# im2col on one core: the first load split by channel over the SyncE and the ScalarE queue, ahead of the opening barrier

## Chip, cores, metric

One core of one Trainium2 chip. The metric is device time in microseconds, the lower the better.

## The reference

The input is `x`, 16 images of 64 channels of 32x32 float32. For each image, channel and tap (ki, kj) of a 3x3 window, the output row holds the 30x30 shifted plane:

```python
for i in range(h_out):            # 30
    for j in range(w_out):        # 30
        patch = x[b, :, i:i + 3, j:j + 3]
        cols[b, :, i * w_out + j] = patch.ravel()      # cols: 16 x 576 x 900
```

There is no arithmetic, only copies. 4.19 MB are read and 33.18 MB written.

## The kernel before

1024 channels lie on 128 partitions, eight channels on each. Four pairs of channels are expanded one after the other into an output tile (two buffers) by VectorE and ScalarE, and each pair goes out as one store of 8.3 MB.

```python
    def load(r0, r1):
        return nc.sync.dma_start(out=in_flat[:, r0 * W : r1 * W],
                                 in_=x_v[:, r0 * W : r1 * W])

    first = load(0, 2 * H)        # channels 0 and 1: 8192 bytes per partition
    load(2 * H, CPP * H)          # channels 2 to 7: 24,576 bytes per partition
    ...
    for c in range(0, CPP, 2):    # four pairs
        out_tile = out_pool.tile([P, 2, KK, HO, WO], x.dtype, name="out_tile")
        for s in range(2):
            ...                   # ScalarE: taps 3..5 (and 8 if s == 1); VectorE: the rest
        nc.sync.dma_start(out=..., in_=...)     # 64,800 bytes per partition
    ...
    # after compilation: 'first' is moved ahead of SyncE's drain in the opening barrier
```

## Time and profile before

| | before |
|---|---|
| device time, median of 3 runs | 91.12 us |
| span in the profile (that run took 91.39 us) | 89.6 us |
| first packet starts, last store packet ends | 1.01 us, 88.33 us |
| first pair of channels: copies start | 4.93 us |
| first store issued | 10.69 us |

The span runs from the first to the last instruction; device time is 1.8 us more.

A landing is counted from the issue and includes the time in which a transfer stands behind others. Where the text speaks of "packets", it means the trace's single DMA records: start, duration, queue and bytes of each. A row of one partition is one packet: the trace of before has 128 of either load and 512 of the stores, on the mean of the 16 DMA engines eight of each load and 32 store packets.

### The profile page before, as it was taken

Reading aid. Unit: us, or ns where it says so; the run is one execution under the profiler, and the core shown is the slowest. Engines: PE = TensorE matmul, PEld = TensorE weight load, DVE = VectorE, ACT = ScalarE, POOL = GpSimd, SP = SyncE. Lnnn points to the kernel's source line nnn. Section 1 sums busy time; section 2 is a strip of 40 time slices with the busy share of each in tenths; the row PEclk is TensorE's granted clock in tenths of the full one; section 3 lists DMA queues with packets and bytes.
Section 4 is the critical chain, followed back from the end, with each engine's and each line's share of the span. In section 5 each row is a group of like instructions: output and inputs, shape, how many; then the busy total and the mean of one; then the engine's idle time right before and its main releaser. Section 6 shows DMA issues by size and latency. Waiting matters only on the chain.

```text
span 89.6 us, 96 instructions
## 1 busy us (share of the span) xinstructions
DVE 22.6 (25%) x24; ACT 23.8 (27%) x13; POOL 0.2 (0%) x4
## 2 busy tenths in 40 slices
DVE  0079759900000099500000399100000000000000
ACT  5079759900000099500000399100000000000000
POOL 0000000000000000000000000000000000000000
DMA  5989899999999999947999999999999982999990
GB/s 128 505 384 494 362 463 463 463 463 463 463 463 463 463 463 463 434 174 318 463 463 463 463 463 463 463 463 463 463 463 463 463 347 116 463 463 463 463 463 0
DMA packets 864, 37.37 MB, mean 417 GB/s; under 512 B 96, under 2 KB 96, under 8 KB 96
## 3 DMA queue, kind: packets, MB, share of 16 engines
q1 hardware_dynamic: 864, 37.37, 97.2%
HBM read 4.19 MB, written 33.18 MB: 417 GB/s over the span
## 4 chain that ended last, share of the span: by engine, by line
DMA 49%; DVE 12%; DVEq 1%; issue 0%; SPq 0%
DMA out_dram<-out_tile 36%; DMA in_tile<-in_x_dram 13%; DVE out_tile L57 8%; DVE out_tile L61 2%; DVE out_tile L65 1%; DVEq L89 1%; DVEq L57 0%; SPq L71 0%
## 5 line engine op out<-in xcount | busy, mean ns | idle before, releaser
L55 ACT COPY out_tile<-in_tile 128x2700 f32<-128x2700 f32 x8 | 19.2, 2443 | 31.7 <-DMA out_dram<-out_tile 27.1
L57 DVE COPY out_tile<-in_tile 128x1800 f32<-128x1800 f32 x16 | 16.8, 1092 | 33.7 <-DMA out_dram<-out_tile 27.1
L61 DVE COPY out_tile<-in_tile 128x1800 f32<-128x1800 f32 x4 | 4.4, 1090 | 0.0
L68 ACT COPY out_tile<-in_tile 128x900 f32<-128x900 f32 x4 | 3.8, 938 | 0.0
L65 DVE COPY out_tile<-in_tile 128x900 f32<-128x900 f32 x4 | 2.5, 620 | 0.0
L55 ACT ACT_TABLE_LOAD x1 | 1.3, 1283 | 0.8 <-PEq L118 0.8
L118 POOL MEMSET const-bfloat16-1.0<- 128x1 bf16 x1 | 0.1, 101 | 0.0
L118 POOL MEMSET const-uint8-127<- 128x1 uint8 x1 | 0.1, 101 | 0.0
L118 POOL MEMSET const-float32-0.0<- 128x1 f32 x1 | 0.1, 98 | 0.2 <-issue 0.2
L118 POOL MEMSET const-float32-1.0<- 128x1 f32 x1 | 0.1, 98 | 0.0
## 6 DMA issues: line engine op xcount, KB each, us to landing
out_dram<-out_tile SPq DMA_DIRECT2D x4, 8100.0 KB, 32.4
in_tile<-in_x_dram SPq DMA_DIRECT2D x1, 3072.0 KB, 11.4
in_tile<-in_x_dram SPq DMA_DIRECT2D x1, 1024.0 KB, 4.9
```

The costliest lines, as they stand in the source:

```text
L55: nc.scalar.copy(out=o[:, K : 2 * K], in_=planes(c + s, 1, 0, K, 1))
L57: nc.vector.tensor_copy(out=o[:, ki * K : ki * K + 2], in_=planes(c + s, ki, 0, 2, 1))
L61: nc.vector.tensor_copy(out=o[:, 2:KK:6], in_=planes(c + s, 0, 2, 2, 2 * W))
L65: nc.vector.tensor_copy(out=o[:, 2], in_=in_tile[:, c + s, 0:HO, 2 : 2 + WO])
L68: nc.scalar.copy(out=o[:, 8], in_=in_tile[:, c + s, 2 : 2 + HO, 2 : 2 + WO])
L89: tc.compile()
L118: nc = _bacc.Bacc("TRN2", target_bir_lowering=False, num_devices=1)
```

## The change

The intent is to have channel 0 in SBUF earlier: two loads of 512 KB, on two queues, both out before the barrier, so that the copies and the first store can start sooner.

```diff
-    def load(r0, r1):
-        return nc.sync.dma_start(
+    def load(queue, r0, r1):
+        return queue.dma_start(
...
-    first = load(0, 2 * H)
-    load(2 * H, CPP * H)
+    first = load(nc.sync, 0, H), load(nc.scalar, H, 2 * H)
+    load(nc.sync, 2 * H, CPP * H)
...
-    load = first.ins
-    (moved ahead of the drain of its engine in the first block)
+    for load in (f.ins for f in first):
+        (the same, each ahead of the drain of its own engine)
```

More of the change, by code (lines that the diff above doesn't have):

```diff
@@ L90 @@
     blocks = tc.nc.main_func.blocks
-    load = first.ins
-    home = next(b for b in blocks if any(i.name == load.name for i in b.instructions))
-    home.instructions = [i for i in home.instructions if i.name != load.name]
-    head = list(blocks[0].instructions)
-    at = next(
-        k
-        for k, i in enumerate(head)
-        if i.engine == load.engine and type(i).__name__ == "InstDrain"
-    )
-    head.insert(at, load)
-    blocks[0].instructions = head
+    for load in (f.ins for f in first):
+        home = next(
+            b for b in blocks if any(i.name == load.name for i in b.instructions)
+        )
+        home.instructions = [i for i in home.instructions if i.name != load.name]
+        head = list(blocks[0].instructions)
+        at = next(
+            k
+            for k, i in enumerate(head)
+            if i.engine == load.engine and type(i).__name__ == "InstDrain"
+        )
+        head.insert(at, load)
+        blocks[0].instructions = head
 _INS = ['x', 'kernel_size']
```

## The prediction

> **What bounds the kernel now.** I read the page's busy shares first, then its DMA queue, then the chain of waits, and last the timeline of the first 18 us and the trace's single DMA packets, because the change touches only the first five microseconds.
>
> The queue table and the busy line say which resource is full:
>
> ```profile
> DVE 22.6 (25%) x24; ACT 23.8 (27%) x13; POOL 0.2 (0%) x4
> ...
> q1 hardware_dynamic: 864, 37.37, 97.2%
> HBM read 4.19 MB, written 33.18 MB: 417 GB/s over the span
> ```
>
> VectorE and ScalarE work a quarter of the span each; the 16 DMA engines are busy for 97.2% of it. That leaves 2.8% of 89.6 us, 2.5 us per DMA engine, in which no packet moves. This is all that any change of order can win. The packet records say where those 2.5 us lie. The first packet starts at 1.01 us (the 16 engines start one after the other until 1.39), the last store packet ends at 88.33, so about 1.0 to 1.4 us lie at the head and 1.27 at the tail. In between each engine works almost without a pause. The dips in the GB/s row near 40 and 74 us are no idle time: in the records a new row of 16 packets starts within 6 ns of the old one's end there.
>
> The one inner gap is between the loads and the first store. On the engine that is done first the second load ends at 11.25 us and its first store packet starts at 11.54, a gap of 0.29 us; on the last engine they are at 11.839 and 11.836, no gap. The mean over the 16 engines is about 0.18 us (loads end at 11.42 on average, stores start at 11.6).
>
> The timeline shows how the first store comes to be issued when it is:
>
> ```profile
> 0.00 1.12 SPq L35 DMA_DIRECT2D in_tile<-in_x_dram  x2
> ...
> 0.78 1.28 ACT L55 ACT_TABLE_LOAD   x1 [0.78 <-PEq L118]
> 4.93 4.79 ACT L55 COPY out_tile<-in_tile 128x2700 f32<-128x2700 f32 x2 [2.87 <-DMA in_tile<-in_x_dram]
> 4.93 2.10 DVE L57 COPY out_tile<-in_tile 128x1800 f32<-128x1800 f32 x2 [4.93 <-DMA in_tile<-in_x_dram]
> ...
> 9.63 0.94 ACT L68 COPY out_tile<-in_tile 128x900 f32<-128x900 f32 x1
> 9.97 0.62 DVE L65 COPY out_tile<-in_tile 128x900 f32<-128x900 f32 x1
> 10.69 7.60 SPq L71 DMA_DIRECT2D out_dram<-out_tile  x2
> ```
>
> Both engines wait for the first load until 4.93 and then work without a break until 10.57 (ScalarE) and 10.59 (VectorE). The store is issued at 10.69; its first packet follows 0.85 us later, at 11.54. The second load holds the DMA engines until 11.24 to 11.83 meanwhile. So the compute of the first pair of channels is already hidden under the second load, all but that gap of 0.29 us. The page's chain names the second load, and then the stores, as what ended last:
>
> ```profile
> DMA 49%; DVE 12%; DVEq 1%; issue 0%; SPq 0%
> DMA out_dram<-out_tile 36%; DMA in_tile<-in_x_dram 13%; DVE out_tile L57 8%; DVE out_tile L61 2%; DVE out_tile L65 1%; DVEq L89 1%; DVEq L57 0%; SPq L71 0%
> ```
>
> Its VectorE share is misleading: it lies under store packets (the compute of 50.6 to 56.3 us runs beside the third store). What sets the end is the packet stream, 32 store packets per engine at a pace of 2.395 us, 76.6 us, from 11.6 to 88.3.
>
> [...] 64,800 bytes each 2.395 us on 16 engines is 433 GB/s[...].
>
> **The change part by part.** It takes 4 KB per partition from the first load and gives them to the ScalarE queue. Bytes, copies and stores stay.
>
> *Packets.* Eight packets of 8192 bytes per engine, 306 ns apart, become sixteen of 4096. From the paces of 306 ns and 908 ns (24,576 bytes) a packet costs about 5 ns plus 36.7 ns per 1024 bytes, so 4096 bytes take about 155 ns (an estimate); 16 x 155 - 8 x 306 is +0.03 to +0.04 us on the stream.
>
> *Issue.* SyncE issues at 0.00 as before. ScalarE's first recorded instruction, the drain of the barrier, is at 0.13 us, so its load goes out near 0.13[...]. SyncE's own drain runs from 0.43 to 0.56 and lets the barrier go (second load at 0.79). ScalarE's drain then comes last, so the second load is issued at about 0.9 to 1.1. That costs nothing: the rings are full until after 3.5 us. The table load moves by as much and ends at 2.4 at the latest, before any data.
>
> *Landing of channel 0.* The data of both first loads take the same time together, to 3.98 to 4.56 us. If both rings fill at once and alternate, channel 0 is complete one packet before channel 1, so 0.15 us earlier than now. If ScalarE's packets come 0.3 us later, SyncE's ring leads by two or three packets, and channel 0 is complete some 0.3 to 0.5 us earlier. The copies start at about 4.5 to 4.8.
>
> *Landing of channel 1.* SyncE's ring goes straight on with packets of 24,576 bytes, 0.91 us each. [...] ScalarE needs it 2.35 us after its start, at 6.9 to 7.2; VectorE 3.03 us after. [...]
>
> *First store.* Its issue moves from 10.69 to between 10.2 and 10.7. What that is worth is capped by the gap, 0.18 us on average, since the second load ends no earlier. I take -0.08 us for it, +0.04 for the packets, and -0.03 for a start in which two first packets per engine overlap (now the first packet takes 0.51 to 1.15 us instead of 0.31). The sum is -0.07, so 91.12 becomes 91.05. One more semaphore in the closing waits falls in SyncE's idle time.
>
> **The rivals.**
>
> *Channel 1 is starved.* If the ScalarE ring starts a microsecond late, [...] Channel 1 then lands near 8.7 to 9, is visible near 9.2, ScalarE needs 3.3 us after that (2.35 + 0.94), and the store is issued at 12.5: its packets come at 13.4 instead of 11.6, and nothing fills the hole. This makes 92.5 to 93. For it: the order within SyncE's ring. Against it: ScalarE reaches the barrier at 0.13 us already, so it is not late.
>
> *Channel 0 really comes first.* If the rings are not served in turn but SyncE's first, channel 0 lands near 3.1 and the copies start 1.2 us earlier. The store is issued before 10, the gap closes fully, and the time is 90.9. Even this best case wins no more than the 0.2 us, because the copies are hidden by the second load anyway.
>
> *The start is faster.* Two queues could halve the ramp of 0.38 us in which the engines begin, or hide the slow first packets. Every store then starts up to 0.4 us earlier, if the first store is issued as much earlier too: 90.7. Against it: both queues feed the same engines[...].
>
> **Range and chances.** The ordinary outcomes lie between 90.9 and 91.2; three runs of before spread over 0.11 us. I widen down to 90.75 for the faster start and up to 91.5 for a channel 1 that comes late by about half a microsecond. Faster by 2% would need 89.3 us, which is 1.8 us out of 2.5 us of idle time of which the tail keeps 1.27: 1%. Slower by 2% is 92.94, the hard form of starvation: 3%. Within 2%: 96%.
>
> **What would show it.** In the profile after: a second hardware queue in the DMA table, with the sum of both shares again near 97%; two first loads of 512 KB whose landings differ by less than 2.5 us; the copies starting at 4.5 to 4.8; no wait of ScalarE or VectorE for a load between the channels of over 0.5 us; the first store issued at 10.2 to 10.7. A landing of ScalarE's load after 8 us, or a first store after 11, would prove the step on channel 1 wrong. A first packet before 0.8 us, or copies from 4.0 on, would prove the step on the start wrong.

-0.08, +0.04 and -0.03 make the -0.07 that takes 91.12 to 91.05. The -0.03 is the author's estimate, from the first packets' 0.51 to 1.15 us, for an overlap that he had not measured. The 8.7 to 9 us of the first rival and the half microsecond in the range stand as his estimates, and so does the lateness of 0.3 us under channel 0, an assumption.

## More of the kernel before

One more view of the kernel before, its DMA issues (what goes where, the issuing queue, how many, KB each, microseconds from issue to landing):

```profile
out_dram<-out_tile SPq DMA_DIRECT2D x4, 8100.0 KB, 32.4
in_tile<-in_x_dram SPq DMA_DIRECT2D x1, 3072.0 KB, 11.4
in_tile<-in_x_dram SPq DMA_DIRECT2D x1, 1024.0 KB, 4.9
```

## The result

The changed kernel took 91.41 us (median of 6 runs, 91.34 to 91.55), the kernel before 91.19 (6 runs, 91.10 to 91.30). The ratio is 1.0026, 95% interval 1.0013 to 1.0038. (Ratios here are the mean time of one kernel's runs over that of the other's in the same rounds, so not quite the ratio of the medians quoted.) Executions over 1.5% slower than the fastest of the same kernel are left out of the means. It is 0.2 us slower, clear of noise but far inside 2%. The predicted 91.05 lay on the other side of the kernel before.

The profile after shows that the change did what it was meant to do. Its timeline up to the first store (start, duration, engine, line, operation; in brackets the idle time before and what ended it):

```profile
0.00 1.24 SPq L35 DMA_DIRECT2D in_tile<-in_x_dram  x2
0.12 0.37 ACTq L35 DMA_DIRECT2D in_tile<-in_x_dram  x1
...
0.90 1.28 ACT L55 ACT_TABLE_LOAD   x1 [0.90 <-PEq L120]
4.23 4.79 ACT L55 COPY out_tile<-in_tile 128x2700 f32<-128x2700 f32 x2 [2.04 <-DMA in_tile<-in_x_dram]
4.23 2.10 DVE L57 COPY out_tile<-in_tile 128x1800 f32<-128x1800 f32 x2 [4.23 <-DMA in_tile<-in_x_dram]
...
9.27 0.62 DVE L65 COPY out_tile<-in_tile 128x900 f32<-128x900 f32 x1
9.98 8.25 SPq L71 DMA_DIRECT2D out_dram<-out_tile  x2
```

The copies start at 4.23 instead of 4.93 and the first store is issued at 9.98 instead of 10.69: 0.7 us won. The second half arrives in time, so ScalarE runs its two first copies without a break (4.79 us for both, as before). The DMA tables of the same profile, queues (packets, MB, share of 16 engines' span) and issues:

```profile
q1 hardware_dynamic: 864, 36.85, 95.6%
q10 hardware_dynamic: 144, 0.52, 1.5%
...
in_tile<-in_x_dram SPq DMA_DIRECT2D x1, 3072.0 KB, 11.2
in_tile<-in_x_dram SPq DMA_DIRECT2D x1, 512.0 KB, 4.2
in_tile<-in_x_dram ACTq DMA_DIRECT2D x1, 512.0 KB, 4.7
```

The shares add up to 97.1%, against 97.2% before, and never more than 16 packets of both queues together run at once, as with one queue before: the second queue brought no further DMA engines. The large load was issued at 0.91 and landed 11.2 us later, at 12.13, against 12.19 before. The chain of waits after begins as before with that load and goes on with the stores (start, duration, what):

```profile
0.91 11.22 DMA in_tile<-in_x_dram
...
17.89 32.58 DMA out_dram<-out_tile
```

So 0.7 us at the first copy have vanished by the end of the loads. And the two profiles hide the result: both spans are 89.6 us. The profiled run of before, 91.39 us, was slower than that kernel's six timed runs; the one of after, 91.34, was the fastest of its six. Where a fifth of a microsecond is at stake, one profile per kernel is not a comparison. What both profiles share is more useful. Apart from the gap before the first store, the packets of loads and stores follow each other on a DMA engine almost without a pause (the shares of 97.1% and 97.2% above). The records do not name the engine, but there are 16 last packets of the loads, and in the profile after one of the 16 first store packets starts 2 to 3 ns after the end of each. So they are taken as one per engine, and the latest of them is the end of the loads on the slowest engine:

| profiled run | loads end, mean of 16 engines | loads end, slowest engine | last store packet ends | difference of the last two | device time of that run |
|---|---|---|---|---|---|
| before | 11.45 | 11.83 | 88.33 | 76.5 | 91.39 |
| after | 11.50 | 11.76 | 88.26 | 76.5 | 91.34 |
| after, again | 11.78 | 12.18 | 88.64 | 76.5 | 91.75 |
| first store early | 11.46 | 11.82 | 88.31 | 76.5 | 91.42 |
| split on SyncE alone | 12.26 | 13.85 | 90.30 | 76.4 | 93.39 |

The end is the slowest engine's end of loads plus 76.4 to 76.7 us, in all 14 profiles; that is 32 store packets at 2.39 us. Device time is 79.5 to 79.7 us after the same moment. In the kernel before, this slowest engine has no gap (its loads end at 11.834, and the last of the 16 first store packets starts at 11.836), though most of the others have one; the mean gap of all 16 is 0.15 us.

### The profile page after: what moved, and what is told of

Its sections match the earlier page's. It is cut to its first block, busy times and chain, and to the rows that moved or that the text cites. A ratio compares the mean times of both kernels' runs of the same rounds, so it can differ in the third digit from the quotient of the medians.

```text
span 89.6 us, 97 instructions
## 1 busy us (share of the span) xinstructions
DVE 22.6 (25%) x24; ACT 23.8 (27%) x13; POOL 0.2 (0%) x4
## 3 DMA queue, kind: packets, MB, share of 16 engines
HBM read 4.19 MB, written 33.18 MB: 417 GB/s over the span
## 4 chain that ended last, share of the span: by engine, by line
DMA 49%; DVE 12%; DVEq 1%; issue 0%; SPq 0%
DMA out_dram<-out_tile 36%; DMA in_tile<-in_x_dram 13%; DVE out_tile L57 8%; DVE out_tile L61 2%; DVE out_tile L65 1%; DVEq L89 1%; DVEq L57 0%; SPq L71 0%
## 6 DMA issues: line engine op xcount, KB each, us to landing
in_tile<-in_x_dram SPq DMA_DIRECT2D x1, 3072.0 KB, 11.2
```

## The experiments

Three theories stood after the result. Q: a second queue in use has a fixed price. S: the split costs time in the packet stream, through smaller packets or through the order in the rings. N: it is the difference of chips and rounds.

### The changed kernel again

No edit but a comment.

> The changed kernel once more, for spans of both kernels on one chip. Theory Q (a second queue in use has a fixed price): again 0.15 to 0.3 us slower than before. Theory S (the split itself, with smaller packets and the changed order in the rings, costs time in the packet stream): the same time, but seen inside the span. Rival N (difference of chips and rounds): within 0.1 us of before, with an interval that holds 1.

91.66 us (91.41 to 91.75), before 91.32 (91.17 to 91.48), ratio 1.0032, interval 1.0018 to 1.0046. N falls: the loss is there again, with both kernels timed side by side on one chip. The spans of these runs are 89.6 to 90.0, those of before 89.4 to 89.7, so it lies inside the span.

### A second queue that is idle at the start

```diff
+        if c == 0:
+            nc.scalar.dma_start(out=spare, in_=x_v[0:16, 0:16])
```

> The kernel before with its loads untouched, plus one load of 16 rows of 64 bytes on the ScalarE queue into a spare buffer that nobody reads, issued after the first pair's copies. It carries 1 KB, so the packet stream is unchanged. Theory Q: 0.15 to 0.3 us slower than before, with the same packet stream. Theory S: within 0.1 us of before.

91.30 us against 91.32, ratio 0.9998 (0.9985 to 1.0010). Q falls. The profile shows something else about rings: the little load was issued at 4.87 us and its packets ran between 8.5 and 9.0, after four more packets of 0.91 us from SyncE's ring on every engine.

### The queues swapped

```diff
-    first = load(nc.sync, 0, H), load(nc.scalar, H, 2 * H)
+    first = load(nc.scalar, 0, H), load(nc.sync, H, 2 * H)
```

> The changed kernel with the queues swapped: channel 0 on ScalarE, channel 1 on SyncE. In the changed kernel ScalarE's ring sent its first packet 1.2 us after SyncE's though the issue came only 0.12 us later. If that is the ring's own late start, channel 0 now lands last, near 4.5, and the copies start at 4.85 to 4.95 as before the change; the first store goes out near 10.7. Theory Q: 0.15 to 0.3 slower than before. If the early first store is worth something, this is slower than the changed kernel by up to 0.2.

91.44 us, ratio 1.0015 (1.0003 to 1.0028). The copies start at 4.93 and the first store is issued at 10.69, exactly as in the kernel before, so ScalarE's ring is the late one: in the changed kernel its first packet starts at 2.24 us although it was issued at 0.12, while SyncE's starts at 1.02. That the first store is 0.7 us later than in the changed kernel did not make the kernel slower than that one; the time is even lower, by an amount that the two intervals do not separate.

### The first store early, with the loads untouched

```diff
+            cut = c == 0 and s == 1
+            if cut:
+                nc.gpsimd.memset(o[:, 2], 0.0)
+                nc.gpsimd.memset(o[:, 8], 0.0)
...
-            else:
+            elif not cut:                      # the last copy of either engine
```

The result is wrong (taps 2 and 8 of channel 1 on every partition are zero).

> The kernel before with its loads untouched, and the last copy of the first pair on either engine taken away; GpSimd writes zeros there instead, so the result is wrong on purpose. The first store goes out near 9.8 instead of 10.69, early enough to close the gap on every DMA engine. The prediction's step (the mean gap of 0.18 us counts, at least 0.08 of it): 0.08 to 0.18 us faster than before. The rival (the end is the slowest DMA engine's end of loads plus a constant 76.5 us, and that engine has no gap): within 0.05 us of before, the spread of the engines at the end 0.4 to 0.6 us instead of 0.18.

91.33 us against 91.24, ratio 1.0009 (0.9996 to 1.0021). The timeline of this run:

```profile
4.92 4.79 ACT L59 COPY out_tile<-in_tile 128x2700 f32<-128x2700 f32 x2 [2.86 <-DMA in_tile<-in_x_dram]
...
7.95 2.09 DVE L61 COPY out_tile<-in_tile 128x1800 f32<-128x1800 f32 x2
10.14 0.35 SPq L75 DMA_DIRECT2D out_dram<-out_tile  x1
```

VectorE was busy until 10.0, so the store went out at 10.14, not near 9.8. That is early enough: on every engine the first store packet starts 2 to 3 ns after the end of the loads, from 11.165 on the first engine to 11.824 on the last. The gap is closed and nothing is won, since the last engine never had one. Its lead lets the first engine end earlier, and the spread at the end is 0.67 us instead of 0.18, a little more than the rival expected (0.4 to 0.6). This is where the intended gain of the change goes: a first store earlier than about 10.7 us fills gaps on engines that then wait for the slowest one at the end.

### The split on SyncE alone

```diff
-    first = load(nc.sync, 0, H), load(nc.scalar, H, 2 * H)
+    first = load(nc.sync, 0, H), load(nc.sync, H, 2 * H)
```

> The same split into two loads of one channel ahead of the barrier, but both on the SyncE queue. Theory Q: no second queue, so no price: 91.0 to 91.2, as before or 0.1 faster. Theory S: 0.15 to 0.3 slower than before, as the change is. Channel 0 should land first by 1.2 us in the profile (copies from 3.7 to 3.9), because one ring keeps its order.

93.29 us (92.59 to 93.50), ratio 1.0204 (1.0178 to 1.0230), much slower than either theory allowed. The timeline:

```profile
0.00 1.58 SPq L35 DMA_DIRECT2D in_tile<-in_x_dram  x3
...
3.68 4.79 ACT L55 COPY out_tile<-in_tile 128x2700 f32<-128x2700 f32 x2 [1.14 <-DMA in_tile<-in_x_dram]
...
9.44 0.35 SPq L71 DMA_DIRECT2D out_dram<-out_tile  x1
14.17 1.10 DVE L57 COPY out_tile<-in_tile 128x1800 f32<-128x1800 f32 x1 [4.83 <-DMA in_tile<-in_x_dram]
```

Channel 0 comes 1.25 us earlier than before (copies from 3.68 against 4.93), so the ring kept its order here; the first store is issued at 9.44, and yet the second pair waits for the large load until 14.17 instead of 12.21. The packet records show where the time goes: packets of 24,576 bytes, 0.912 us each in the kernel before without one exception, took up to 2.0 us, on many engines, between 4 and 13 us. Over all engines they lost 0.43 us each on the mean, and the slowest engine lost 2.1. The two earliest first stores of the whole study, this one and 9.41 in the second load after the barrier (below), go with two of its slowest kernels.

### The same once more, reversed, and with the second load after the barrier

Unchanged:

> The SyncE-only split once more, unchanged. It was 2% slower than before because packets of the second load (24,576 bytes) took up to 2.0 us instead of 0.91, on several DMA engines, between 4 and 12.5 us. Theory A (chance of where this build's tensors lay): now 91.1 to 91.5, all large packets 0.91. Theory B (a property of the order): again 92.5 to 93.5 with such packets.

Ratio 1.0148 (1.0091 to 1.0206), four runs of 91.80 to 93.67 us (93.67 is counted as slow and is not in the ratio). Theory A falls: another build is slow again, and its loads end at 13.56 us on the slowest engine (13.85 in the first, 11.83 before).

Copies of channel 1 first:

```diff
-        for s in range(2):
+        for s in ((1, 0) if c == 0 else (0, 1)):
```

> The SyncE-only split with the first pair's copies done for channel 1 first, then channel 0. Channel 1 lands second, so the copies start at 4.8 to 5.0 as before the change instead of 3.7, with the same three loads. Theory C (copies that start before the large packets do slow these down): 91.1 to 91.5. Theory D (three loads queued on one ring ahead of time slow the large packets down, whatever the copies do): 92.5 to 93.5.

92.41 us, ratio 1.0129 (1.0109 to 1.0150). Copies start at 4.97, the large packets are slow all the same, 0.64 us per engine on the mean. Theory C falls.

On the kernel before:

```diff
-    first = load(0, 2 * H)
+    first = load(0, H)
+    load(H, 2 * H)
```

> All three loads on SyncE, but only channel 0 ahead of the barrier; channel 1 and the rest after it. Theory C: copies again start near 3.7, so again slow, 92.5 to 93.5. Theory D: the loads are issued later (near 0.8 and 1.15 us), the last one at about the time of the slow kernel, so it should be slow too; if the time is 91.1 to 91.4, both fall and the issue ahead of the barrier matters.

93.38 us, ratio 1.0229 (1.0204 to 1.0254). It is not the issue ahead of the barrier. D stands.

### A third load on the ring that carries nothing

```diff
     first = load(0, 2 * H)
+    nc.sync.dma_start(out=spare, in_=x_v[0:16, 0:16])
     load(2 * H, CPP * H)
```

> The kernel before with one load of 1 KB (16 rows of 64 bytes, into a spare buffer) on the SyncE queue between its two loads; the second load is issued near 1.17 us as in the slow kernels. If three loads queued on one ring, or the later issue of the last, slow the large packets: 92.3 to 93.5 and packets of over 1 us between 4 and 8 us. If it takes small packets too, or the split: within 0.1 of before.

92.36 us, ratio 1.0129 (1.0110 to 1.0148). The issues of this run:

```profile
in_tile<-in_x_dram SPq DMA_DIRECT2D x1, 3072.0 KB, 11.9
in_tile<-in_x_dram SPq DMA_DIRECT2D x1, 1024.0 KB, 4.6
spare<-in_x_dram SPq DMA_DIRECT2D x1, 1.0 KB, 4.0
```

A load of 1 KB makes the large one, which is unchanged, land 0.5 us later after its issue, and the issue itself is 0.4 us later (1.19 us). Stage by stage, the kernel before and then this one (window, length, busy time of VectorE, ScalarE, GpSimd, clock, mean busy share of the DMA engines, GB/s):

```profile
2.50:4.00 1.50, 0.00 (x0) 0.00 (x0) 0.00 (x0) 1.00 1.07 453
4.00:8.00 4.00, 3.07 (x4) 3.07 (x2) 0.00 (x0) 1.00 1.10 475
```

```profile
2.50:4.00 1.50, 0.00 (x0) 0.00 (x0) 0.00 (x0) 1.00 1.09 453
4.00:8.00 4.00, 3.41 (x4) 3.41 (x2) 0.00 (x0) 1.00 0.97 350
```

A share over 1 comes from counting a packet in one window; read the two rows against each other. Up to 4 us the streams are equal. In the next 4 us the kernel with three loads moves 350 GB/s, a quarter less, while its DMA engines still count as busy: the packets are longer (up to 1.85 us), and some engines also stand idle for a while before their first large packet. So small packets are not needed for it. Whether it is the number of loads on the ring or the late issue of the last one was not separated by a run of its own: the issue is at 1.17 to 1.26 us in the five slow kernels and at 0.92 at the latest in the undisturbed ones with two loads on the ring. One run speaks for the number: in the halves by partition, below, the large load goes out at 1.48 us as the second on its ring, and its packets take 0.91 to 0.93 us once the small loads are through.

### Small packets without a split

One load on SyncE, as before, into a buffer with a spare row behind each channel:

```diff
-    first = load(0, 2 * H)
+    first = nc.sync.dma_start(
+        out=pair.rearrange("p c h w -> p c (h w)")[:, :, 0 : H * W],   # pair: [P, 2, H + 1, W]
+        in_=x_v[:, 0 : 2 * H * W].rearrange("p (c n) -> p c n", c=2))
```

> One first load on SyncE as before, but into a buffer with a spare row behind each channel, so that it consists of packets of 4096 bytes instead of 8192. Nothing else changes. Theory P (the doubled number of packets in the cold head costs): small packets end about 0.15 to 0.2 us later on the mean, the time 0.15 to 0.3 above before. Theory R (the second ring costs): within 0.06 of before. If the large packets become slow (92 or more), it is small packets ahead of them on the same ring that slow them, not the number of loads.

91.38 us against 91.24, ratio 1.0010 (0.9995 to 1.0026). The last small packet ends at 4.22 us on the mean of the engines, against 4.18 before. The large packets stay at 0.912. So the small packets cost something like 0.04 to 0.1 us, which the interval does not part from zero. They are probably not the whole, but the upper end of the interval, 0.26%, just reaches the ratio of the change.

### Halves by partition

```diff
-    first = load(nc.sync, 0, H), load(nc.scalar, H, 2 * H)
+    first = (load(nc.sync, 0, 2 * H, slice(0, 64)), load(nc.scalar, 0, 2 * H, slice(64, 128)))
```

> Two first loads on SyncE and ScalarE as in the change, but split by partitions (64 each), so every packet stays at 8192 bytes. Each DMA engine gets four packets from either ring. Theory R: 0.15 to 0.3 us above before. Theory P: within 0.06 of before. Both halves are needed by the first copy, so copies start near 4.9 and the store goes out near 10.7.

93.82 us, ratio 1.0283 (1.0262 to 1.0303): a failed test, as the split brought a cost of its own. Issues and the second stage of this run:

```profile
in_tile<-in_x_dram SPq DMA_DIRECT2D x1, 512.0 KB, 5.1
in_tile<-in_x_dram ACTq DMA_DIRECT2D x1, 512.0 KB, 7.3
```

```profile
2.50:4.00 1.50, 0.00 (x0) 0.00 (x0) 0.00 (x0) 1.00 1.09 251
```

The DMA engines count as busy (mean share 1.09, 1.07 before) at 251 GB/s instead of 453. A packet of 8192 bytes takes about 0.61 us instead of 0.309. ScalarE's queue carried 80 packets, 64 rows and 16 of 4 bytes, so four rows per engine on the mean. The two rings ran mostly one after the other (SyncE's packets first; the halves landed 5.1 and 7.3 us after their issues), so most of the time the rows of 64 partitions moved alone. The lower rate is measured here; what sets it was not shown.

### The second ring by itself

The first load whole and on SyncE, and a load of 1 KB on ScalarE ahead of the barrier:

```diff
+    first = (load(nc.sync, 0, 2 * H), nc.scalar.dma_start(out=spare, in_=x_v[0:16, 0:16]))
```

> The kernel before with its first load whole (8192-byte packets), plus one load of 1 KB (16 rows of 64 bytes, into a spare buffer) on the ScalarE queue ahead of the barrier, as early as the changed kernel issues its second half. The run with split packets on one ring left about 0.2 us of the change's cost unexplained; the partition halves did not test the second ring, because they ran at half the rate. Theory R (a second ring that starts in the cold head costs by itself): 0.15 to 0.3 us above before, and the slowest engine's end of loads later by as much. Rival T (it costs only by its data, that is by the alternation of small packets, or by both together): within 0.08 us of before. The barrier goes 0.12 us later in either case, which should cost nothing.

91.36 us against 91.26, ratio 1.0005 (0.9991 to 1.0019). A second ring that starts in the first microseconds and brings next to no data costs nothing that could be told from noise. Theory R is unlikely: of its 0.15 to 0.3 us the interval allows 0.17 at most, and the slowest engine's end of loads, 11.78 us, is not later than before (11.83). The later barrier (the large load is issued at 0.91 instead of 0.79) is in this run too, and hides in the same noise.

### What is left of the 0.2 to 0.3 us

Small packets in one load came to 0.10% and a second ring without data to 0.05%, neither clear of zero; the change came to 0.26% and 0.32%. What they have not and the change has is that the data of the first pair come as two loads. In the records a packet of 4 bytes follows each engine's share of each load (before has 96 of them, 16 for each of two loads and four stores). Its start gives the time at which an engine has brought in its share of the first pair; here is the mean of the 16 engines, counted from the first issue:

| first pair of channels | profiled runs | first pair in, us | loads end, slowest engine | device time of these runs |
|---|---|---|---|---|
| one load, 8192-byte packets | before, idle queue, early store, second ring empty | 4.18, 4.19, 4.18, 4.19 | 11.83, 11.77, 11.82, 11.78 | 91.39, 91.36, 91.42, 91.36 |
| one load, 4096-byte packets | small packets | 4.22 | 11.78 | 91.50 |
| two loads on two rings | after, again, swapped | 4.21, 4.50, 4.26 | 11.76, 12.18, 11.79 | 91.34, 91.75, 91.40 |
| two loads on one ring (slow large packets) | SyncE alone, again, reversed, second after the barrier | 4.24, 4.24, 4.24, 4.33 | 13.85, 13.56, 13.20, 13.91 | 93.39, 93.08, 92.74, 93.44 |

Of the kernels without slow large packets only the repeat of the change shows the loss: its first pair is in 0.3 us later than before (ScalarE's first packet starts at 2.48 us; in the first profile of the same kernel it was 2.24), and its loads end 0.35 us later on the slowest engine. The first profile of the change and the swapped one come out of the loads no later than the kernel before. So the loss lies before the end of the loads, as device time follows that moment by 79.5 to 79.7 us in every profile; in the one profile that has it, it is there after the first 4.5 us. Whether it comes of two loads as such was not shown: the first pair is in later with two loads in six of seven profiles, but mostly by 0.02 to 0.08 us, one profile per kernel. Nor is it excluded that small costs add up: the point estimates for small packets, second ring and early store (0.09%) come to 0.24% together, and each interval includes zero. The cause of the 0.2 to 0.3 us stays open.

No version beat the kernel before.

## Why the prediction was right, and which step was not

The time fell into the range, 91.41 in 90.75 to 91.5, and "within 2%" held. The second rests on the right mechanism, the first in part on luck: 91.41 lies above the 90.9 to 91.2 that the prediction called ordinary, and its upper end was set for a channel 1 that comes late, which did not happen. In the repeat the same kernel took 91.66, outside the range, with the kernel before at 91.32. The forecast of 0.07 us faster had the wrong sign. Two slips in its working change little: the loads end at 11.45 on average and not at 11.42, so the mean gap is 0.15 us and not 0.18, and "36.7 ns per 1024 bytes" is per 1000 bytes (its 155 ns for 4096 bytes is right: it is the distance of two such packets most often found in the trace after). By its steps:

- **The bound.** Right. The packet stream sets the end, and the copies of the first pair (done at 9.89 us) are hidden under the second load (until 11.76). The DMA shares add up to 97.1%, as asked for.
- **Issue and barrier.** Right. ScalarE's load went out at 0.12, the large load at 0.91 (forecast 0.9 to 1.1), and the run with an empty second ring shows that this costs nothing clear of noise (ratio 1.0005).
- **Landing of channel 0 and the first store.** The size was missed on the good side: copies from 4.23 rather than 4.5 to 4.8, and the store at 9.98, ahead of the forecast 10.2 to 10.7. The rings do not alternate from the start. 66 of the 128 packets on SyncE's ring, four per engine on the mean, started before ScalarE's first at 2.24 us; until 3.71 us its other 62 ran mixed with 86 of ScalarE's; and ScalarE's last 42 started after that.
- **Landing of channel 1.** The lateness that the forecast feared did not come: when the first large packet started, at 3.96 us, only 19 of ScalarE's 128 packets were still to start, and the last of them ended at 4.49. ScalarE's ring did start a microsecond late (2.24 us against 1.02), the condition of the starvation rival, without that rival's consequence.
- **"I take -0.08 us for it".** This is the step that failed. It valued the gap between loads and stores by its mean over the engines, as 0.08 of 0.18 us, though the prediction itself had noted that the last engine has no gap. The kernel ends with its slowest engine. The early store measured by itself is worth nothing (ratio 1.0009). With the value from the slowest engine, the term is 0.
- **"+0.04 for the packets" and "-0.03 for a start in which two first packets per engine overlap".** Together about 0; measured was +0.24 to +0.29 us for the change as a whole (0.26% and 0.32% of 91.2). The packets alone measured +0.10% (-0.05 to 0.26%), about 0.09 us, which the +0.04 fits. With the term above at 0, these two leave +0.01, so some 0.2 to 0.3 us have no term in the sum. Which of the two is mis-sized, or what is missing, is not shown; in the one profile that has the loss the first pair came in 0.3 us later, where the start was to be 0.03 faster.
- **The rivals.** "Channel 0 really comes first" happened in half (0.7 us of 1.2) and showed its own limit, that such a lead is worth nothing here (early store: ratio 1.0009), more strictly than it said. "The start is faster" did not happen: first packets at 1.02 us as before.

## What to carry to other kernels

Where a stream runs on many DMA engines without a pause, ask for the slowest engine, not for the mean: closing a gap that it does not have was worth nothing here (ratio 1.0009). Before a load is made to land earlier, look at whether the work behind it is hidden already; if it is, as here, there is nothing to win. And when splitting a load, count the loads queued on one ring and the partitions that each part spans: here a third load on the ring cost 1.3 to 2.3%, a split into halves of 64 partitions 2.8%.

## Measured here, but not explained

- A second ring got its first turn only after some rows that the first had in hand: about four of 4096 bytes per engine in the changed kernel (first packet at 2.24 us against 1.02, issued 0.12 us apart), four of 24,576 bytes with the idle queue (issued at 4.87, served from 8.5). What sets it was not tested.
- With three loads queued on one ring the packets of the last one became slow: up to 2.0 us in the split on SyncE alone and 1.85 with the load of 1 KB, instead of 0.912 for 24,576 bytes, at 1.3 to 2.3% of the time. What does it stays open.
- The two first issues of the changed kernel overlap (0.00 to 0.385 and 0.12 to 0.486 us) and each takes 0.37 to 0.39 us, as one alone does (0.38 before); neither is seen to wait for the other. In the halves by partition the two overlapping issues take 0.55 and 0.54 us; why was not tested.
- In the kernel before, the first packet starts 1.0 us after the start of the first issue and 0.85 us after that of the first store; counted from the end of the issue it is 0.63 and 0.50 us. The first packet of 8192 bytes on each engine takes 0.51 to 1.15 us instead of 0.309.
